# State-space stage: GpSimd's work for a quarter of the channels dealt out over the tiles ahead of it, and ScalarE's copies of output matrices placed behind the next tile's inputs

## The chip, the cores and the metric

The kernel runs on one core of one Trainium2 chip, in one launch. The metric is the device time in microseconds (us). The core has five engines with a queue each: TensorE (PE in the rows, PEld its weight loads), VectorE (DVE), ScalarE (ACT), GpSimd (POOL) and SyncE (SP), which issues most of the transfers.

## The reference, cut to what matters

Two layers on x (256 positions, 2048 channels). The first layer's token mixer is a state-space model (S5): 128 groups of 16 channels, each with 64 complex states.

```python
a_bar = exp(lam * dt)
b_bar = ((a_bar - 1) / lam) * b_mat
bu = einsum('btgi,gpi->btgp', u, b_bar)
h  = scan of  h[t] = a_bar * h[t-1] + bu[t]
y  = real(einsum('btgp,gip->btgi', h, c_mat))
y  = gelu(y + d_skip * u);  vg = y @ w_glu
...
mod = silu(c) @ ada_w[i] + ada_b[i]        # six conditioning vectors for each layer
x = layer_norm(ALPHA*x + (1+gate)*sublayer(x*(1+scale)+shift))
```

A SwiGLU feed-forward follows, then a second layer with a convolution mixer in place of S5. Only the S5 part is touched by the change.

## The kernel before, in words

The 2048 channels are 16 tiles of 128 channels (`ct`), in 4 quarters of 4 tiles. The state-space stage is a loop over the tiles, pipelined by hand over three of them. Iteration `ct` does these things in program order:

- `weights_in(ct+1)`: ScalarE copies input matrices (`mb`, L376), TensorE transposes them (`btr`, L384), ScalarE copies the result (`lz`, L385).
- `ada_units`: TensorE multiplies 1 MB units of the conditioning weights that stream in (`ada`, L613). `plan` gives a tile 2, 3 or 4 units; they stand between the other steps. A finished block of four units is copied (`adas`, L616) and turned (`adat`, L620).
- `tables(ct+1)`: ScalarE copies a tile's part of the quarter's table `tq` into `tab` (L358), and GpSimd doubles it once more (L349).
- `read_out(ct-1)`: TensorE computes `y` (L476 to L487) from the state that VectorE left (`pc`, `psn`).
- `inputs(ct+1)`: TensorE transposes x (`xt`), ScalarE applies the conditioning (`uh` and `u`, L930) and last scales X (L1297). `drive(ct+1)`: TensorE multiplies `uh` into `pin` (L421).
- `weights_out(ct+1)`: five ScalarE instructions, one `dd` (L393) and four that copy the output matrices `qc` into `mc` (L396, L397, two each); then TensorE's `bdp` (L399, L403), which reads them, and ScalarE's `bd` (L407). `mc` and `dd` have three buffers.
- `scan(ct)`: VectorE's chain over `pin` (L438 to L471), with the gelu of tile ct-1 between its steps: ScalarE L1304, VectorE L1307, ScalarE L1308, VectorE L1312 (`gl`), ScalarE L1313 (`h`), GpSimd L1314.
- GpSimd's work for the next quarter, queued behind its own last instruction of `tables(ct+1)`. `matrices(q)` has three steps (L311), each of four multiplications and two sums over 128x256; the first makes `qb` for `weights_in`, the other two `qc` for `weights_out`. `quarter(q)` makes `tq` in five doublings j = 0 to 4 (L349), each twice as wide as the one before.

TensorE's instructions run in the order of the program (a manual schedule). On the other engines the build's scheduler chooses the order among instructions whose inputs it holds ready, and the order is fixed in the program. `issue_after(ins)` places what a block issues on that instruction's engine behind it in the queue; it is not a wait for its end. Each engine's queue runs in its order.

In the kernel before, `matrices(1)` takes one step in each of the iterations 0, 1 and 2, and `quarter(1)` is issued whole behind the second step. For quarters 2 and 3 the steps stand in iterations 3, 4, 5 and 7, 8, 9, and the whole `quarter` behind the third step, in iterations 5 and 9. The `weights_out` instructions of ScalarE stand behind the X scaling of tile 0 alone (`first`).

Of the kernel before, what the change touches and what calls it, by code (L numbers as in the profile page):

```python
# [153 lines left out]
class S5:  # L154
# [170 lines left out]
    def quarter(self, q, eng):  # L325

        t = self.tq[q] = self.keep.tile([P, 2, 16, 32], F32, tag="tq", name="tq", bufs=2)
        sl = slice(16 * q, 16 * q + 16)
        for r in range(2):
            eng.memset(t[:, r, :, 0:1], 1.0 - r)  # L330
        xt, yt = (self.keep.tile([P, 2, 16, 16], F32, tag=n, name=n) for n in ("xq", "yq"))
        for j in range(5):
            self.double(t, self.wt[:, j, :, sl], j, xt, yt, 16, eng)

    def double(self, t, w, j, xt, yt, npair, v):

        n = 1 << j
        src = t[:, :, :, 0:n]
        if n == 1:
            src, xs, ys = t[:, :, :, 0], xt[:, :, :, 0], yt[:, :, :, 0]  # L340
            f = [bc(w[:, r, :], 1, 2) for r in range(2)]
        else:
            xs, ys = xt[:, :, :, 0:n], yt[:, :, :, 0:n]
            f = [bc(bc(w[:, r, :], 1, 2), 3, n) for r in range(2)]
        parts = [(xs, src, f[0], MUL), (ys, src, f[1], MUL),
                 (t[:, 0, :, n:2 * n], xt[:, 0, :, 0:n], yt[:, 1, :, 0:n], SUB),
                 (t[:, 1, :, n:2 * n], xt[:, 1, :, 0:n], yt[:, 0, :, 0:n], ADD)]
        for out, a, b, op in parts:
            last = v.tensor_tensor(out=out, in0=a, in1=b, op=op)  # L349
        return last  # L350
# [143 lines left out]
def kernel(  # L494
# [9 lines left out]
    nc = tc.nc  # L504
# [6 lines left out]
    def aux(name):  # L511
        return auxp.tile([P, 512], F32, tag="aux", name=name)
# [31 lines left out]
    s5 = S5(tc, const, ident, auxp, "aux", pin_ctx.enter_context(tc.tile_pool(name="pin", bufs=2, space=PSUM)))  # L544
# [51 lines left out]
    def queue_behind(instructions):  # L596

        st = ExitStack()
        for i in instructions:
            st.enter_context(tc.issue_after(i.ins))  # L600
        return st
# [629 lines left out]
    def ada_units(n):  # L1231
        nonlocal block
        for _ in range(n):
            ada_turn()
            if not block:
                if not parts:
                    return
                block = [ada_block(0, *parts.pop(0)), 0]
            next(block[0])
            block[1] += 1  # L1240
# [6 lines left out]
            ada_units(1)  # L1247
    for _ in s5.matrices(0, nc.vector):
        pass
    s5.quarter(0, nc.vector)  # L1250
    s5_prep.close()
    s5.start_work()
    w = s5.work
# [1 line left out]
    def load_x(q):  # L1255
        for t in range(2):
            nc.sync.dma_start(
                X.rearrange("c k (t p) -> c k t p", t=2)[:, 4 * q:4 * q + 4, t],
                x[0].rearrange("(c two) (k p) -> two c k p", two=2, p=P)[t][:, 4 * q:4 * q + 4])
# [3 lines left out]
    d_col, cb_col, cg_col, cnb_col = (vec[:, 16 * i:16 * i + 16] for i in range(4))  # L1263
# [6 lines left out]
    def half_mod(q):  # L1270
        while len(parts) > 12 - 2 * q or block and len(parts) == 12 - 2 * q and block[1] < 4:
            ada_units(1)
        ada_turn()
        s4 = slice(4 * q, 4 * q + 4)
        b = aux("hmod")
        for h in range(2):
            nc.tensor.matmul(b[:, 8 * h:8 * h + 8], s5.sel[:, 2 * h:2 * h + 2].rearrange("p a t b -> p (a t b)"), mod[0][:, 0:2, s4], start=h == 0, stop=h == 1)
        return nc.scalar.copy(out=hmod[:, :, :, s4], in_=b[:, 0:16].rearrange("p (h j k) -> p h j k", h=2, j=2))

    def inputs(ct):  # L1280

        b = aux("xt")
        xc = X[:, ct].rearrange("c (t p) -> c t p", t=2)
        for t in range(2):
            nc.tensor.transpose(b[:, t * P:(t + 1) * P], xc[:, t], ident)
        for h in range(2):
            for i in range(4):
                o, a = 64 * h + 32 * (i // 2), 32 * i
                nc.tensor.matmul(b[a:a + 32, (2 + h) * P:(3 + h) * P], xc[:, i % 2, o:o + 32], ident, start=True, stop=True)
        if ct % 4 == 0 and ct:  # L1290
            half_mod(ct // 4)
        u = w.tile([P, SEQ], F32, tag="u", name="u", bufs=3)
        uh = w.tile([P, 2, HALF], F32, tag="uh", name="uh", bufs=2)
        for h in range(2):
            affine(uh[:, h], b[:, (2 + h) * P:(3 + h) * P], hmod[:, h, 1, ct:ct + 1], hmod[:, h, 0, ct:ct + 1])
        affine(u, b[:, :SEQ], mod[0][:, 1, ct:ct + 1], mod[0][:, 0, ct:ct + 1])
        return u, uh, nc.scalar.mul(X[:, ct], b[:, :SEQ], ALPHA)  # L1297
# [18 lines left out]

        return first, second, third

    extra = s5.matrices(1, nc.gpsimd)
    tabs, held, coming = {}, None, None  # L1320
    more = ExitStack()
    raws[:] = [rawp] * 4 + [more.enter_context(tc.tile_pool(name="raw5", bufs=2))] * 2
# [2 lines left out]
    def start_dense():  # L1325
        nonlocal const2, wp
        const2 = ctx.enter_context(tc.tile_pool(name="const2", bufs=1, reuse_waits="tile"))
        wp = mctx.enter_context(tc.tile_pool(name="w", bufs=2, reuse_waits="tile"))
        ready.append(Unit(wp, s5_w_glu[0], 0, 4, [(0, 256), (D, 256)]))
# [3 lines left out]
    def scan(ct, now, y):  # L1333

        nonlocal held
        turns = list(gelu(*held[:2], y)) if held else []

        def between():
            if turns:
                turns.pop(0)()  # L1340

        held = ct, now[1], *s5.scan(ct, now[2], tabs.pop(ct), between)
        while turns:
            between()

    with tc.manual_schedule(engines={mybir.EngineType.PE}):
        half_mod(0)
        first = None
        for ct in range(-1, NCH - 1):
            now, y = coming, None  # L1350
            if (ct + 1) % 4 == 1 and ct < 12:
                load_x(ct // 4 + 1)
            s5.weights_in(ct + 1)
            n = plan[ct + 1]
            ada_units(n > 0 and ct >= 0)
            tabs[ct + 1] = s5.tables(ct + 1)
            if held:
                y = s5.read_out(*held)
            u, uh, last = inputs(ct + 1)
            first = first or last  # L1360
            ada_units(n > 1 and ct >= 0)
            coming = ct + 1, u, s5.drive(ct + 1, uh)
            s5.weights_out(ct + 1, d_col[:, ct + 1:ct + 2], first)
            ada_units(n - 2 if ct >= 0 else n)
            if ct == NCH - 2:
                raws[:] = [rawp]
                more.close()
                s5.keep_ctx.close()
                start_dense()
            if ct < 0:  # L1370
                continue
            scan(ct, now, y)
            if ct % 4 == 3 and ct < 11:
                extra = s5.matrices(ct // 4 + 2, nc.gpsimd)
            with queue_behind([s5.last]):
                next(extra, None)
                if ct % 4 == 1 and ct < 12:
                    s5.quarter(ct // 4 + 1, nc.gpsimd)
    accp = None

    def last_scan():
# [57 lines left out]
    with mctx:  # L1439
# [18 lines left out]
        first = {"acc": [b.rearrange("p (a b) -> p a b", b=SEQ) for b in (aux("acc"), bank)], "before": {1: last_scan, 2: lambda: held_back.append(s5.end), 3: s5_end}}  # L1458
# [180 lines left out]
```

## Time and profile before

| | |
|---|---|
| runs | 2353.70, 2355.54, 2361.51 us; median 2355.54 us |
| profiled execution | 2354.07 us, of which the span from first to last instruction is 2352.3 us |
| mean granted TensorE clock | 0.986 of full |
| the stage's VectorE chain, first instruction of tile 0 to last of tile 14 | 48.80 to 232.84 us, 184.04 us |

The span is the part of the time that the rows can show. The stage is less than a tenth of it; matrix products with streamed weights follow up to the end.

### The profile page before, as it was taken

To read this page: it belongs to the slowest core of one execution; us is meant where nothing else is said; L and a number is where in the kernel's file an instruction comes from. 1 tells how busy PE (TensorE), PEld (TensorE's weight loads), DVE (VectorE), ACT (ScalarE), POOL (GpSimd) and SP (SyncE) were. 2 spreads that over 40 slices of the span, in tenths; PEclk is the share of its full clock that TensorE was granted. 3 is DMA by queue.
4 is the path that set the end of the run, shared out by engine and by line. 5 is a ranking of instruction groups with operands and counts; after the bars stand their busy time and mean duration, and the time that the engine had idled before them with its cause. 6 is when DMAs were issued, how large, how long until landed. Compare 5 with 4: busy or idle time off the path is not lost.

```text
span 2352.3 us, 34010 instructions
## 1 busy us (share of the span) xinstructions
PE 2264.1 (96%) x13837; PEld 1825.5 (78%) x13837; DVE 1643.2 (70%) x1790; ACT 1014.1 (43%) x1239; POOL 227.7 (10%) x290
## 2 busy tenths in 40 slices
PE   6788999999999999999999999899999999999999
PEld 4454877888888888888887767797888888888888
DVE  8889988878777777777885555888755544454564
ACT  4566334553433333433453322556434333344343
POOL 2673000200000000000031101402000000000000
PEclk9899999999999999999999999999999999999998
DMA  9678799588888898988746776775875555555542
GB/s 349 239 266 303 257 338 350 166 283 307 305 307 305 315 315 295 322 304 308 276 146 202 222 230 209 274 242 163 281 235 189 187 186 189 188 188 182 194 162 89
DMA packets 378546, 580.29 MB, mean 247 GB/s; under 512 B 14835, under 2 KB 272163, under 8 KB 363923
## 3 DMA queue, kind: packets, MB, share of 16 engines
q1 hardware_dynamic: 377958, 577.68, 71.6%
q8 instruction: 108, 1.77, 0.3%
q0 software_dynamic: 192, 0.37, 0.1%
q14 instruction: 48, 0.39, 0.0%
q10 hardware_dynamic: 240, 0.08, 0.0%
HBM read 567.83 MB, written 2.10 MB: 242 GB/s over the span
## 4 chain that ended last, share of the span: by engine, by line
PE 75%; issue 7%; DVE 6%; POOL 6%; ACT 3%; DMA 3%; SPq 1%; POOLq 0%; DVEq 0%; ACTq 0%
PE acc L869 64%; PE acc L873 3%; PE conv L1535 2%; DVE wlo L816 2%; PE turned L885 2%; ACT whi L815 1%; POOL h L967 1%; DMA raw<-in_cv_w_pw_dram 1%; POOL mu L311 1%; DMA raw<-in_s_w_glu_dram 1%; SPq L1518 1%; DVE adaacc L684 1%; POOL tq L349 0%; DVE pin L450 0%; POOL hf L1574 0%
## 5 line engine op out<-in xcount | busy, mean ns | idle before, releaser
L816 DVE TENSOR_TENSOR wlo<-raw,whi 128x2048 fp32r<-128x2048 f32 x344 | 797.5, 2319 | 507.4 <-ACT whi L815 490.6
L815 ACT CAST whi<-raw 128x2048 fp32r<-128x2048 f32 x344 | 654.9, 1904 | 829.2 <-PE acc L869 561.4
L869 PE MATMUL acc<-whi,h 128*128 128x512 f32 x3648 | 899.7, 396 | 15.9 <-ACT whi L815 15.3
L869 PEld LDWEIGHTS acc<-whi,h 128*128 128x128 f32 x3648 | 681.2, 189 | 176.9 <-ACT whi L815 24.4
L869 PE MATMUL acc<-wlo,h 128*128 128x512 f32 x1824 | 465.6, 393 | 3.6 <-DVE wlo L816 3.6
L869 PEld LDWEIGHTS acc<-wlo,h 128*128 128x128 f32 x1824 | 343.0, 188 | 80.8 <-DVE wlo L816 5.9
L869 PE MATMUL acc<-whi,f 128*128 128x512 f32 x1248 | 300.5, 391 | 0.0
L684 DVE SCALAR_TENSOR_TENSOR adaacc<-rawa,c_act,adaacc 128x2048 f32<-128x2048 f32 (+1 forms) x135 | 287.1, 2127 | 0.4
L869 PEld LDWEIGHTS acc<-whi,f 128*128 128x128 f32 x1248 | 233.2, 188 | 48.8 <-ACT whi L815 0.8
L869 PE MATMUL acc<-wlo,f 128*128 128x512 f32 x624 | 156.5, 389 | 0.0
L869 PEld LDWEIGHTS acc<-wlo,f 128*128 128x128 f32 x624 | 117.2, 188 | 24.2
L1507 POOL TENSOR_TENSOR lw<-fold,wtap 128x1024 f32<-128x1024 f32 x16 | 35.6, 2229 | 897.4 <-PE acc L873 710.6
L967 POOL TENSOR_TENSOR h<-hf,h 128x512 fp32r<-128x512 f32 x24 | 48.2, 2016 | 329.9 <-ACT h L966 322.6
L613 PE MATMUL ada<-raw,c_rep 128*32 128x512 f32 x512 | 72.9, 659 | 6.7 <-DVE c_rep L559 4.8
L1192 ACT ACTIVATE fsg<-acc 128x256 f32<-128x256 f32 x84 | 31.9, 380 | 104.5 <-PE acc L869 104.5
L873 PEld LDWEIGHTS acc<-h,whi 128*128 128x128 f32 x512 | 62.3, 190 | 9.5 <-DVE h L1564 2.9
L1138 POOL CAST lnmh<-lno 128x2 fp32r<-128x2 f32 x1 | 0.2, 182 | 713.8 <-DVE lno L65 713.8
L873 PE MATMUL acc<-h,whi 128*128 128x256 f32 x512 | 66.3, 285 | 2.8 <-DVE h L1564 2.0
L1535 PE MATMUL conv<-vs,lw 128*32 128x256 f32 x1024 | 62.8, 380 | 0.0
L1535 PEld LDWEIGHTS conv<-vs,lw 128*32 128x32 f32 x1024 | 41.7, 109 | 16.6 <-issue 3.5
L1193 DVE TENSOR_TENSOR fsg<-acc,fsg 128x256 f32<-128x256 f32 x84 | 35.3, 420 | 19.9 <-ACT fsg L1192 19.8
L450 DVE TENSOR_TENSOR_SCAN pin<-rho,pin 128x256 f32<-128x256 f32 x64 | 44.3, 692 | 1.3
(334 smaller groups left out, 1853.4 us busy)
## 6 DMA issues: line engine op xcount, KB each, us to landing
raw<-in_ffn_w_gu_dram SPq DMA_DIRECT2D x352, 512.0 KB, 4.4
rawa<-in_ada_w_dram SPq DMA_DIRECT2D x128, 1024.0 KB, 5.6
raw<-in_ffn_w_down_dram SPq DMA_DIRECT2D x88, 1024.0 KB, 5.0
raw<-in_ada_w_dram SPq DMA_DIRECT2D x64, 1024.0 KB, 7.3
raw<-in_s_w_glu_dram SPq DMA_DIRECT2D x64, 512.0 KB, 5.9
raw<-in_cv_w_pw_dram SPq DMA_DIRECT2D x64, 512.0 KB, 4.9
raw<-in_cv_w_pw_dram SPq DMA_DIRECT2D x16, 1024.0 KB, 5.5
vs<-pad SPq DMA_DIRECT2D x112, 71.0 KB, 2.1
```

What stands on the lines that cost most here:

```text
L450: v.tensor_tensor_scan(out=z, data0=rh[:, a].rearrange("p r h c -> p (r h c)"), data1=z, initial=0.0, op0=MUL, op1=ADD)
L613: nc.tensor.matmul(acc[32 * k:32 * k + 32, :], c_rep[:, 4 * u + k, :], r[:, k, :], start=u == 0, stop=u == 3)
L684: nc.vector.scalar_tensor_tensor(out=acc, in0=r[:, i], scalar=c_act[:, kk:kk + 1], in1=acc, op0=MUL, op1=ADD)
L815: m1 = nc.scalar.copy(out=self.hi[:, :kn], in_=r[:, :kn])
L816: m2 = nc.vector.tensor_tensor(out=self.lo[:, :kn], in0=r[:, :kn], in1=self.hi[:, :kn].bitcast(F32), op=SUB)
L869: nc.tensor.matmul(acc[bank].rearrange("p a b -> p (a b)"), x[:, bank * HALF:(bank + 1) * HALF], wt[:, k], start=first, stop=end)
L873: nc.tensor.matmul(acc[bank][:, i], wt[:, k, m * P:(m + 1) * P], x, start=first and i == 0, stop=end and i == 1)
L885: nc.tensor.transpose(b[:, o:o + HALF], u[t][:, c0 + k * P:c0 + (k + 1) * P], ident)
L967: nc.gpsimd.tensor_tensor(out=hl[:, s2], in0=h, in1=hh[:, s2].bitcast(F32), op=SUB)
L1193: nc.vector.tensor_tensor(out=t[:, i], in0=gv[:, 0], in1=t[:, i], op=MUL)
L1507: nc.gpsimd.tensor_tensor(out=lw, in0=fold32.unsqueeze(1).unsqueeze(1).broadcast_to([P, 4, CONV_G, 32]), in1=bc(wtap[:, :, 4 * ch:4 * ch + ...
L1535: nc.tensor.matmul(acc[32 * q:32 * q + 32, :], lw[:, q, g, :], vs[:, q, 4 * g:4 * g + SEQ], start=g == 0, stop=g == CONV_G - 1)
```

## The change

`quarter` becomes a generator that stops after each doubling. A new generator, `quarter_steps(q)`, deals out the three matrix steps `m` and the five doublings `t`. For quarters 2 and 3 this is over four iterations: m; m; m and three doublings; the last two doublings. For quarter 1 it is over three iterations: two m; m and three doublings; two doublings. Besides, `weights_out(ct+1)` now stands behind the X scaling of its own tile's inputs (`last`), where it stood behind that of tile 0. No instruction is added or taken away.

```diff
--- before.py
+++ after.py
@@ -331,6 +331,7 @@
         xt, yt = (self.keep.tile([P, 2, 16, 16], F32, tag=n, name=n) for n in ("xq", "yq"))
         for j in range(5):
             self.double(t, self.wt[:, j, :, sl], j, xt, yt, 16, eng)
+            yield
 
     def double(self, t, w, j, xt, yt, npair, v):
 
@@ -1247,7 +1248,8 @@
             ada_units(1)
     for _ in s5.matrices(0, nc.vector):
         pass
-    s5.quarter(0, nc.vector)
+    for _ in s5.quarter(0, nc.vector):
+        pass
     s5_prep.close()
     s5.start_work()
     w = s5.work
@@ -1316,7 +1318,15 @@
 
         return first, second, third
 
-    extra = s5.matrices(1, nc.gpsimd)
+    def quarter_steps(q):
+
+        m, t = s5.matrices(q, nc.gpsimd), s5.quarter(q, nc.gpsimd)
+        for steps in ((m,), (m,), (m, t, t, t), (t, t)) if q > 1 else ((m, m), (m, t, t, t), (t, t)):
+            for g in steps:
+                next(g)
+            yield
+
+    extra = quarter_steps(1)
     tabs, held, coming = {}, None, None
     more = ExitStack()
     raws[:] = [rawp] * 4 + [more.enter_context(tc.tile_pool(name="raw5", bufs=2))] * 2
@@ -1345,7 +1355,6 @@
 
     with tc.manual_schedule(engines={mybir.EngineType.PE}):
         half_mod(0)
-        first = None
         for ct in range(-1, NCH - 1):
             now, y = coming, None
             if (ct + 1) % 4 == 1 and ct < 12:
@@ -1357,10 +1366,9 @@
             if held:
                 y = s5.read_out(*held)
             u, uh, last = inputs(ct + 1)
-            first = first or last
             ada_units(n > 1 and ct >= 0)
             coming = ct + 1, u, s5.drive(ct + 1, uh)
-            s5.weights_out(ct + 1, d_col[:, ct + 1:ct + 2], first)
+            s5.weights_out(ct + 1, d_col[:, ct + 1:ct + 2], last)
             ada_units(n - 2 if ct >= 0 else n)
             if ct == NCH - 2:
                 raws[:] = [rawp]
@@ -1371,11 +1379,9 @@
                 continue
             scan(ct, now, y)
             if ct % 4 == 3 and ct < 11:
-                extra = s5.matrices(ct // 4 + 2, nc.gpsimd)
+                extra = quarter_steps(ct // 4 + 2)
             with queue_behind([s5.last]):
                 next(extra, None)
-                if ct % 4 == 1 and ct < 12:
-                    s5.quarter(ct // 4 + 1, nc.gpsimd)
     accp = None
 
     def last_scan():
```

## Rows read from the trace of the kernel before

**Rows 1.** By stretch: us; busy PE, PEld, DVE, ACT, POOL; PEclk; DMA share; GB/s

```profile
48.80:232.84 184.04, 150.41 (x2251) 88.59 (x2251) 160.43 (x338) 118.95 (x349) 103.36 (x203) 0.93 0.79 277
...
287.00:411.00 124.00, 121.24 (x548) 94.06 (x547) 105.54 (x89) 49.57 (x46) 0.00 (x0) 1.00 0.99 343
```

**Rows 2.** Waits of VectorE in the stage: us in total, times, longest us

```profile
DVE gl L1312 <- ACT u L1308: 8.9, 3, 8.5
...
DVE u L1307 <- ACT u L1304: 5.0, 8, 1.3
...
DVE x L438 <- POOL tab L349: 3.6, 2, 1.8
...
DVE gl L1312 <- POOL h L1314: 0.4, 2, 0.2
```

**Rows 3.** VectorE in order of time (start us, us) around its longest wait

```profile
75.35 1.42 DVE L450 TENSOR_TENSOR_SCAN pin<-rho,pin 128x256 f32<-128x256 f32 x2
...
85.29 0.42 DVE L1312 TENSOR_TENSOR gl<-u,y 128x256 f32<-128x256 f32 x1 [8.52 <-ACT u L1308]
```

**Rows 4.** ScalarE in order of time over the same stretch

```profile
72.17 0.38 ACT L1304 ACTIVATE u<-y 128x256 f32<-128x256 f32 x1
...
81.90 0.63 ACT L397 ACTIVATE mc<-qc 64x128 f32<-64x128 f32 x2 [9.36 <-POOL qc L311]
...
82.89 0.80 ACT L930 ACTIVATE uh<-xt,hmod 128x128 f32<-128x128 f32 x2
...
84.04 0.37 ACT L1297 ACTIVATE X<-xt 128x256 f32<-128x256 f32 x1
...
84.77 0.43 ACT L1308 ACTIVATE u<-u 128x256 f32<-128x256 f32 x1
```

**Rows 5.** GpSimd in order of time, second quarter's work and the doublings

```profile
51.83 2.36 POOL L311 TENSOR_TENSOR mu<-cm,par 128x256 f32<-128x256 f32 x4
...
60.42 0.61 POOL L349 TENSOR_TENSOR xt<-tab,wt 128x256 f32<-128x256 f32 x1 [4.85 <-ACT tab L358]
...
62.52 2.36 POOL L311 TENSOR_TENSOR mu<-cm,par 128x256 f32<-128x256 f32 x4
...
66.19 0.17 POOL L330 MEMSET tq<- 128x16 f32 x2
...
70.30 0.63 POOL L349 TENSOR_TENSOR xq<-tq,wt 128x256 f32<-128x256 f32 x1
...
74.71 1.41 POOL L349 TENSOR_TENSOR tq<-xq,yq 128x256 f32<-128x256 f32 x2
...
81.15 1.40 POOL L311 TENSOR_TENSOR qc<-mu,mu 128x256 f32<-128x256 f32 x2
```

**Rows 6.** GpSimd's table and VectorE's wait for it, in the third quarter

```profile
133.97 0.87 POOL L349 TENSOR_TENSOR tab<-xt,yt 128x128 f32<-128x128 f32 x2
...
134.46 0.69 DVE L438 TENSOR_TENSOR x<-pin,tab 128x512 f32<-128x512 f32 x1 [1.79 <-POOL tab L349]
```

**Rows 7.** ScalarE's first tile: start of the five copies, and what follows them

```profile
47.72 0.41 ACT L393 ACTIVATE dd<-ident,vec 128x128 f32<-128x128 f32 x1
...
49.26 0.41 ACT L358 COPY tab<-tq 128x256 f32<-128x256 f32 x1
```

**Rows 8.** TensorE in order of time: transposes of tile 3, `drive` of tile 4

```profile
72.36 0.64 PE L1289 MATMUL xt<-ident,X 128*32 128x128 f32 x16
...
96.82 1.16 PE L421 MATMUL pin<-uh,lz 64*128 64x128 f32 x16
```

**Rows 9.** Busy time by stretch, two tiles with four conditioning units each

```profile
206.99:218.89 11.90, 10.04 (x164) 5.81 (x160) 10.62 (x24) 8.05 (x23) 2.80 (x5) 1.00 0.99 358
...
218.89:229.86 10.97, 10.08 (x164) 5.81 (x160) 10.50 (x25) 5.58 (x17) 3.26 (x6) 1.00 1.05 355
```

**Rows 10.** A small VectorE sum: duration ns min/median/max

```profile
L461 DVE TENSOR_TENSOR cx<-cx,cy x16: 149/156/764, 55.5 to 245.7; 128x4 f32<-128x4 f32 x16
```

**Rows 11.** The load queue's waits in the stage

```profile
SPq L570 <- PE ada L613: 157.8, 44, 14.8
```

## The prediction

> **What bounds the kernel now.** I read the busy time by stretch first. In the stage, VectorE is busy for 160.43 us of 184.04, TensorE for 150.41, ScalarE for 118.95, GpSimd for 103.36 [rows 1]. So VectorE leads with little to spare, TensorE is close behind, and what the stage can give back is VectorE's idle time, 23.6 us. The second view is who VectorE waited for [rows 2]. One wait stands out: 8.5 us of the 8.9 us in which `gl` (L1312) waited for ScalarE's L1308. Next come 5.0 us for L1304 in eight pieces, and 3.6 us in two waits for GpSimd's table. The small rest of the idle time is spread over the gaps between instructions, which the change doesn't touch.
>
> The third view is the order of time around the long wait. VectorE has nothing between the scan that ends at 76.77 and L1312 at 85.29 [rows 3]. ScalarE, which it waits for, stood still from 72.55 to 81.90, and its row names the releaser: the copy `mc` (L397) waited for GpSimd's `qc` (L311) [rows 4]. Behind that copy in ScalarE's queue stood `uh` of tile 3, which TensorE and all the rest wait for, and L1308, which had been ready for long. The copy was for tile 4, one tile ahead of what was needed. And GpSimd was late because its order was two matrix steps, the whole quarter from 66.19 to 76.12, a table, and only then the third matrix step, whose sums start at 81.15 [rows 5]. So a copy that nobody needed yet held up everything behind it.
>
> In quarters 2 and 3 the matrix steps came early enough, but the whole quarter stood in front of a table: GpSimd's two last table instructions start at 133.97, VectorE's `x` waits 1.79 us for them [rows 6]. The pattern stands twice, which gives the 3.6 us.
>
> **The change part by part.** All is set against the profiled execution, 2354.07 us; the median of the runs is 1.47 us above it.
>
> *The long wait, minus 8.5 us.* A matrix step takes GpSimd 3.7 us (62.52 to 66.19, [rows 5]). With two in iteration 0, GpSimd works from 51.83 to about 59.2, and the next table can't start before 60.42 anyway: the pair is free. The third step then follows at 62.5 and ends near 66.2, some 16 us earlier than now. The first three doublings take 66.19 to 70.30, 4.1 us, the last two 70.30 to 76.12, 5.8 us. Tile 3's table then starts when ScalarE has copied its input, just ahead of L1304 in its queue, near 72.4, and takes 2.1 us (60.42 to 62.52). The last two doublings end near 80.3, before tile 4's table is due: that waits for VectorE's tile 2, which after 76.77 still has another scan of 1.42 us [rows 3], its small sums and four turns, so not before 80.3 either, by estimate. ScalarE goes from L1304, done at 72.55, to `uh` when its transposes are there, which the wait didn't hold: 72.36 plus 0.64, 73.0 [rows 8]. From the start of `uh` to the end of X it is 82.89 to 84.41, 1.5 us [rows 4], so X ends near 74.5. The five copies, now behind it, take 1.5 us (47.72 to 49.26, [rows 7]) and L1308 0.43 us: done by 76.6. VectorE asks for it at 76.77. So the whole 8.52 us go, and either half of the change removes most of this wait alone: what would be late next is the other half's wait, some 2 us for the table, which GpSimd finishes now near 78.9 (76.12, one other instruction and the 2.1 us).
>
> *The two table waits, minus 3.6 us.* With two of the five doublings put behind the table, GpSimd is 5.8 us earlier at it, against a wait of 1.79. `pin` isn't late there. With it go the two waits for GpSimd's L1314, minus 0.4 [rows 2], which stood behind the same doublings.
>
> *Copies no longer ahead of L1304 and `uh`, minus 1.3 us.* Copies for a tile ahead stand between `y` and L1304 and cost up to 0.3 us in about half of the tiles. Bounds: nothing, and all of the 5.0 us that VectorE waits for L1304 [rows 2]. Most of the 5.0 is TensorE's own lateness with `y`, so I take a quarter.
>
> *Copies ahead of L1308, plus 1.5 us.* Behind X the five copies are older in the program than L1308 and will stand before it, 1.5 us, of which `uh` and X gain back some 0.6 by starting earlier. In two tiles L1312 already waits some 0.2 us each for L1308, the rest of the 8.9 us [rows 2]; there VectorE would wait 0.9 us more. I reckon with four tiles of that tight order; the bounds are nothing (VectorE has the next tile's `x` to do instead) and 3.6 us; I take less than half, since the order on VectorE is chosen anew.
>
> *TensorE's `bdp` waits for the copies, plus 1.5 us.* The copies were done a tile ahead; now `bdp` stands in TensorE's fixed order right behind `drive`. From the end of `uh` (82.89 plus 0.80) to that of X it is 0.72 us, the copies 1.5, and `drive` hides 1.16 [rows 8]: TensorE idles 1.1 us in each tile, and behind it stand the conditioning units, the next transposes and `y`. With two or three units a tile TensorE has at least that much idle time, in which it waits for VectorE; there it costs nothing while VectorE leads. In tiles 12 to 15, with four units, TensorE is busy 10.04 of 11.90 and 10.08 of 10.97 us [rows 9], so 0.9 to 1.9 us are there to hide 1.1 plus what already waits on ScalarE. I take 0.4 us for each of four tiles; the bounds are nothing and 1.1 each, 4.4.
>
> *The port of GpSimd and VectorE, nothing.* A tiny VectorE sum, L461, takes 149 ns at best and 764 at worst [rows 10], L460 ahead of it likewise; the long ones fall where GpSimd is at work. GpSimd's work for a quarter spreads into a fourth tile, but the whole quarter already ran over into that tile, so I count no change; the bounds are a gain and a loss of 1.2 us for each of three tiles, 3.6. The Trainium skill's page "SBUF — State Buffer", section "Who interferes with whom", says that a VectorE instruction with two inputs in SBUF and a GpSimd instruction that reads SBUF lock each other out for a whole instruction. The trace agrees, with 764 ns against 149; by that rule work on more tiles costs more, which is the third rival below.
>
> Sum: -8.5 - 3.6 - 0.4 - 1.3 + 1.5 + 1.5 = -10.8 us, 2343.3 by the profiled execution, 2344.7 by the median. What follows the stage passes it on: the load queue spends 157.8 us of the stage waiting for TensorE to free buffers [rows 11], so the loads come earlier with the work. The stretch from 287 to 411 us, with transfers at 0.99 of the engines' time [rows 1], starts earlier as a whole.
>
> **The rivals.**
>
> *TensorE becomes the bound, slower.* If the 1.1 us (1.6 at most: the durations without overlap) at `bdp` counts in each of 15 tiles, it is 16 to 24 us against gains of 13.8. At 1.6 it gives plus 10.2, 2365.7. It breaks even at 0.9 us a tile. For it: TensorE's 150.41 of 184.04, in a fixed order. Against: it now waits for VectorE in most tiles. Chance 0.09.
>
> *The gain is swallowed.* The stretch from 287 us is bound by transfers; were the loads' start set by something other than buffers, or were the new order of VectorE's and ScalarE's queues behind the stage worse by as much, the time would stay, near 2355. Against: rows 11. Also here: the scheduler finds another early instruction that holds ScalarE. Chance 0.14.
>
> *The lock.* Each quarter's extra tile pays 1.2 us: 3.6 less gain, 2348.3. For: the doublings move to where the small sums stand. Against: they were there already. Chance 0.13.
>
> **How the numbers follow.** Forecast 0.64 with 2344.7. A measurement of this kernel tells about 0.3% from no change, 7.1 us, so faster means under 2348.5. The lock rival sits on that line, half of it on either side; a part of the forecast, 0.04, with its losses at their bounds, is also no more than the same. Faster 0.64 - 0.04 + 0.07 = 0.67, same 0.04 + 0.06 + 0.14 = 0.24, slower 0.09. The range: all gains with L1304's whole 5.0 and no loss is -17.5, 2338.0 by the median; gains with losses near their bounds (3.6, 4.4 and a part of 3.6) is about -3, 2352.5. It leaves out slower and the half of the swallowed case.
>
> **What would show it.** ScalarE's L397 shows no wait for GpSimd, and VectorE has no idle time over 2 us between 50 and 220. VectorE's `x` never waits for the table. TensorE's `bdp` has a wait of about 1 us for `mc` in each tile. The stage's chain ends near 222 where it ended at 232.84, and the loads-bound stretch begins as much earlier. I am wrong if `x` or L1312 shows new waits of about a us in most tiles, or if the stage's gain is there and the end doesn't move.

## The result, and the profile after

The changed kernel takes 2342.44 us, median of five runs (2339.14 to 2346.13). Its ratio to the kernel before, run beside it, is 0.9934, 95% interval [0.9917, 0.9952]: faster by 0.7%, 13 us between the medians. The forecast was 2344.7 us, range 2338.0 to 2352.5. The profiled execution of the changed kernel is the slowest of its five (2346.13 us, span 2344.4 us), so its end says less than its stage does.

The stage first, by the same cut as [rows 1], from VectorE's first instruction of tile 0 to its last of tile 14; lines of the changed kernel lie one or two further down (L397 is L398 now, L1304 is L1306, L1308 is L1310, L1312 is L1314).

```profile
48.92:222.95 174.03, 151.31 (x2258) 87.92 (x2259) 162.17 (x338) 116.29 (x350) 104.74 (x204) 0.96 0.87 294
```

174.0 us, where it was 184.0. The engines have about the same work as before; what went is idle time of VectorE, 23.6 us then and 11.9 now. Who VectorE waited for says which, against [rows 2]:

```profile
DVE u L1309 <- ACT u L1306: 4.5, 10, 1.1
...
DVE adasum L624 <- PE adat L621: 2.5, 5, 0.7
DVE gl L1314 <- ACT u L1310: 0.6, 1, 0.6
```

No row of a wait for GpSimd is left: neither for a table nor for `h`. Of the 8.9 us of L1312 for ScalarE, 0.6 stand. VectorE around the place of the long wait, against [rows 3]:

```profile
75.99 1.42 DVE L451 TENSOR_TENSOR_SCAN pin<-rho,pin 128x256 f32<-128x256 f32 x2
...
77.61 0.68 DVE L439 TENSOR_TENSOR x<-pin,tab 128x512 f32<-128x512 f32 x1
...
78.55 0.41 DVE L1314 TENSOR_TENSOR gl<-u,y 128x256 f32<-128x256 f32 x1
```

ScalarE over the same stretch, against [rows 4]:

```profile
73.28 0.39 ACT L1306 ACTIVATE u<-y 128x256 f32<-128x256 f32 x1 [0.81 <-PE y L488]
74.23 0.81 ACT L931 ACTIVATE uh<-xt,hmod 128x128 f32<-128x128 f32 x2 [0.56 <-PE xt L1291]
...
75.38 0.39 ACT L1299 ACTIVATE X<-xt 128x256 f32<-128x256 f32 x1
75.64 0.60 ACT L617 COPY adas<-ada 128x512 f32<-128x512 f32 x1
76.11 0.43 ACT L394 ACTIVATE dd<-ident,vec 128x128 f32<-128x128 f32 x1
...
77.35 0.30 ACT L398 ACTIVATE mc<-qc 64x128 f32<-64x128 f32 x1
77.68 0.42 ACT L1310 ACTIVATE u<-u 128x256 f32<-128x256 f32 x1
```

The copies follow X, none waits for GpSimd, and L1310 stands behind them. It ends at 78.10, when VectorE's scan has been over for 0.7 us; VectorE does not idle, since it takes `x` of the next tile first. It can, because GpSimd has that tile's table ready (against [rows 5]):

```profile
57.98 1.43 POOL L311 TENSOR_TENSOR qc<-mu,mu 128x256 f32<-128x256 f32 x2
61.06 0.61 POOL L350 TENSOR_TENSOR xt<-tab,wt 128x256 f32<-128x256 f32 x1 [1.65 <-ACT tab L359]
...
65.48 1.42 POOL L311 TENSOR_TENSOR qc<-mu,mu 128x256 f32<-128x256 f32 x2
...
73.40 0.87 POOL L350 TENSOR_TENSOR tab<-xt,yt 128x128 f32<-128x128 f32 x2
...
78.61 1.41 POOL L350 TENSOR_TENSOR tq<-xq,yq 128x256 f32<-128x256 f32 x2
```

The third matrix step ends at 66.9 and the table at 74.3. TensorE has the new waits that the prediction spoke of, in total, times and longest:

```profile
PE bdp L404 <- ACT mc L397: 5.5, 11, 0.5
PE y L488 <- DVE pc L439: 5.3, 9, 2.1
PE adat L621 <- ACT adas L617: 4.5, 5, 1.4
PE bdp L400 <- ACT dd L394: 1.9, 5, 0.5
```

With two single waits of 0.6 us put down to GpSimd it is 8.6 us at `bdp` over 15 tiles.

Does what follows move with it? The transfers of the next weights, before and after (duration min/median/max in ns, then first and last start):

```profile
L570 SPq DMA_DIRECT2D raw<-in_s_w_glu_dram x64: 367/478/1571, 218.9 to 403.0; - x64
```

```profile
L571 SPq DMA_DIRECT2D raw<-in_s_w_glu_dram x64: 367/497/1380, 207.9 to 392.9; - x64
```

The first load of that queue comes 11.0 us earlier, the last 10.1. The loads-bound stretch starts earlier as a whole and hands the gain on.

For the experiments one landmark serves in all traces: the start of ScalarE's last L1304 (the first gelu step of tile 15), the last figure of its row. Before and after:

```profile
L1304 ACT ACTIVATE u<-y x16: 376/383/384, 64.0 to 254.9; 128x256 f32<-128x256 f32 x16
```

```profile
L1306 ACT ACTIVATE u<-y x16: 384/385/386, 64.9 to 243.2; 128x256 f32<-128x256 f32 x16
```

254.9 and 243.2: 11.7 us. There is one trace of each kernel, so how far this mark varies between executions is not shown; VectorE's last table instructions ahead of the stage start at 48.3 to 48.8 us in all of them, so a difference of half a us says nothing.

The landmark lies behind the first matrix products of the next part of the kernel (`acc`), and what happens there is in it too. A second mark lies ahead of them: the start of TensorE's `y` of tile 13 (`y<-u,bd`, L476). TensorE runs in the program's order, so the same work stands ahead of it in every kernel here, but for the repeats of `bdp`. Before and after, 11.6 us apart:

```profile
222.72 0.49 PE L476 MATMUL y<-u,bd 128*128 128x129 f32 x2
```

```profile
211.17 0.49 PE L477 MATMUL y<-u,bd 128*128 128x129 f32 x2
```

### The profile page after: what moved, and what is told of

Its sections match the earlier page's. It is cut to its first block, busy times and chain, and to the rows that moved or that the text cites. A ratio compares the mean times of both kernels' runs of the same rounds, so it can differ in the third digit from the quotient of the medians.

```text
span 2344.4 us, 34011 instructions
## 1 busy us (share of the span) xinstructions
PE 2262.0 (96%) x13837; PEld 1822.5 (78%) x13837; DVE 1642.7 (70%) x1790; ACT 1011.0 (43%) x1239; POOL 229.1 (10%) x290
## 4 chain that ended last, share of the span: by engine, by line
PE 74%; DVE 8%; issue 6%; DMA 5%; ACT 4%; POOL 2%; SPq 1%; DVEq 0%; ACTq 0%; POOLq 0%
PE acc L870 64%; PE acc L874 3%; DMA raw<-in_cv_w_pw_dram 2%; PE conv L1541 2%; DVE wlo L817 2%; PE turned L886 2%; DMA raw<-in_s_w_glu_dram 1%; ACT whi L816 1%; POOL h L968 1%; DVE pin L451 1%; PE y L488 1%; DVE adaacc L685 1%; PE ada L614 1%; DMA raw<-in_ada_w_dram 1%; DVE x L439 0%
## 5 line engine op out<-in xcount | busy, mean ns | idle before, releaser
L1194 DVE TENSOR_TENSOR fsg<-acc,fsg 128x256 f32<-128x256 f32 x84 | 35.3, 420 | 19.9 <-ACT fsg L1193 19.8
```

The costliest lines, as they stand in the source:

```text
L1194: nc.vector.tensor_tensor(out=t[:, i], in0=gv[:, 0], in1=t[:, i], op=MUL)
```

## The experiments

All of them in one table; the ratios are to the kernel before, run on the same chip beside each. Its median was 2355.54 us beside the change, 2358.58 beside the first four experiments, 2355.33 beside the next four and 2355.68 beside the last three, so the rows are compared by their ratios and not by their medians.

| kernel | `y` of tile 13, us | landmark, us | median, us | ratio to before, 95% |
|---|---|---|---|---|
| before | 222.7 | 254.9 | 2355.54 | |
| the change | 211.2 | 243.2 | 2342.44 | 0.9934 [0.9917, 0.9952] |
| GpSimd's spread alone | 213.3 | 247.1 | 2342.66 | 0.9939 [0.9925, 0.9953] |
| copies behind their own inputs alone | 213.3 | 245.3 | 2340.86 | 0.9934 [0.9921, 0.9948] |
| the change, `bdp` later | 207.6 | 243.5 | 2342.36 | 0.9938 [0.9926, 0.9951] |
| the change, small sums into PSUM | 209.2 | 241.2 | 2339.29 | 0.9921 [0.9908, 0.9935] |
| spread in quarters 2 and 3 alone | 218.6 | 250.8 | 2348.69 | 0.9973 [0.9962, 0.9984] |
| copies of tile 4 alone | 213.1 | 245.3 | 2346.06 | 0.9956 [0.9941, 0.9970] |
| before, small sums into PSUM | 221.3 | 255.1 | 2353.95 | 0.9987 [0.9979, 0.9995] |
| the change, `bdp` later, sums into PSUM | 204.3 | 239.0 | 2339.72 | 0.9925 [0.9911, 0.9939] |
| copies alone, sums into PSUM | 209.3 | 241.3 | 2340.62 | 0.9937 [0.9922, 0.9953] |
| the change, `bdp` three times | 216.1 | 248.4 | 2343.59 (one run) | |
| the change, `bdp` twice | 211.2 | 243.2 | 2343.75 (one run) | |

**Each half alone.** First GpSimd's spread with the copies where they were:

```diff
+        first = None
...
+            first = first or last
...
-            s5.weights_out(ct + 1, d_col[:, ct + 1:ct + 2], last)
+            s5.weights_out(ct + 1, d_col[:, ct + 1:ct + 2], first)
```

> Only GpSimd's work is dealt out; the output-matrix copies stay behind tile 0's inputs, a tile ahead. Landmark for all runs: the start of the last gelu square on ScalarE in the stage, 254.92 us in the kernel before and 243.2 in the changed one. Theory (GpSimd's lateness was the cause of all three long waits, and placing the copies gives about nothing net): VectorE's 8.5 us wait and both 1.79 us waits for the table are gone, the landmark stands at 242 to 245, and the time is 12 us under the kernel before, 2341 to 2345. Rival (the copies' place was the main part): a long wait of ScalarE's copy for GpSimd stays, the landmark is at 248 or later, and the time is within 5 us of the kernel before.

Then the copies with GpSimd's work as before:

```diff
-        first = None
...
-            first = first or last
...
-            s5.weights_out(ct + 1, d_col[:, ct + 1:ct + 2], first)
+            s5.weights_out(ct + 1, d_col[:, ct + 1:ct + 2], last)
```

> Only the copies are placed behind their own tile's inputs; GpSimd's order stays as in the kernel before. Theory: the 8.5 us wait of VectorE shrinks to some 2 us, now for the table that GpSimd finishes near 79; the two waits of 1.79 us stay; the landmark stands at 248 to 250 and the time is 5 to 7 us under the kernel before, 2349. Rival (the copies' place was the main part): the landmark is at 245 or earlier. Rival (GpSimd alone decides): the long wait stays at 7 us or more, the landmark is near 254.

With the spread alone all three waits are gone; the landmark is 247.1, between the theory's band and the rival's; what is lost against the whole change goes partly to L1304, for which VectorE waits 6.1 us in all where it waits 4.5 in the changed kernel. With the copies alone the long wait has become one of 1.44 us, for the table, and the two waits of 1.79 us, which I expected to stay, are gone too. VectorE in that kernel, at the long wait's place and at that of the first of the two:

```profile
78.53 0.69 DVE L438 TENSOR_TENSOR x<-pin,tab 128x512 f32<-128x512 f32 x1 [1.44 <-POOL tab L349]
...
126.47 1.42 DVE L450 TENSOR_TENSOR_SCAN pin<-rho,pin 128x256 f32<-128x256 f32 x2
127.81 0.67 DVE L438 TENSOR_TENSOR x<-pin,tab 128x512 f32<-128x512 f32 x1
```

And GpSimd's table there:

```profile
126.29 0.88 POOL L349 TENSOR_TENSOR tab<-xt,yt 128x128 f32<-128x128 f32 x2
```

The table is done at 127.17. The new order has put `x` behind the tile's second scans, at 127.81; in the kernel before it stood ahead of them and came too early [rows 6]. So the halves are not terms of a sum: 7.8 and 9.6 us of the landmark alone, 11.7 together; 9.5 and 9.4 by `y` of tile 13, 11.6 together; and in the time no difference between them.

**The copies of one tile.** The kernel before, with the five copies of tile 4 alone moved:

```diff
-            s5.weights_out(ct + 1, d_col[:, ct + 1:ct + 2], first)
+            s5.weights_out(ct + 1, d_col[:, ct + 1:ct + 2], last if ct == 3 else first)
```

> The kernel before with one edit: the five copies of output matrices of tile 4 alone stand behind the X scaling of their own tile's inputs; those of all other tiles, and all of GpSimd's work, as before. Theory (one copy, a tile early, held all of ScalarE's queue): the 8.5 us wait shrinks to some 1.4 us for the table, the two waits of 1.79 us for tables in quarters 2 and 3 stay; the last gelu square at 247.8 us (254.9 less 7.1), or 246 if VectorE's new order hides those two as well; the time 2346 to 2348. Rival (the gain of the copies' new place comes from all sixteen tiles, the long wait being only where it shows): the landmark at 251 or later, the time over 2350.

The landmark is 245.3, the same as with the copies of all tiles and 0.7 us beyond the better end of the theory, and the time is 2346.06 us, as the theory had it. VectorE's wait at the old place, and a later one:

```profile
78.82 0.69 DVE L438 TENSOR_TENSOR x<-pin,tab 128x512 f32<-128x512 f32 x1 [1.11 <-POOL tab L349]
...
175.01 0.69 DVE L438 TENSOR_TENSOR x<-pin,tab 128x512 f32<-128x512 f32 x1 [1.13 <-POOL tab L349]
```

8.5 us have become 1.1. Of the two other waits one is left, with 1.13 us. The cause of the long wait is shown: these five copies, a tile ahead of need, in ScalarE's queue in front of `uh` of tile 3.

**The other side of it: only the quarters without the long wait.** Quarter 1's order as before, quarters 2 and 3 spread, copies as before:

```diff
-for steps in ((m,), (m,), (m, t, t, t), (t, t)) if q > 1 else ((m, m), (m, t, t, t), (t, t)):
+for steps in ((m,), (m,), (m, t, t, t), (t, t)) if q > 1 else ((m,), (m, t, t, t, t, t), (m,)):
...
+        first = None
...
+            first = first or last
...
-            s5.weights_out(ct + 1, d_col[:, ct + 1:ct + 2], last)
+            s5.weights_out(ct + 1, d_col[:, ct + 1:ct + 2], first)
```

> Quarter 1's work on GpSimd in the order of before (one step; one step and the whole quarter; one step), quarters 2 and 3 spread as in the changed kernel, ScalarE's copies placed as before. Theory (the long wait of 8.5 us comes from quarter 1's order alone, the two waits of 1.79 us from the whole quarter ahead of the table): VectorE's wait of about 8.5 us near 77 us is there as before, no wait for a table is left; the last gelu square of the stage at about 251 us (254.9 before, less 3.6), the time 2350 to 2353. Rival one (the two table waits are swallowed by the order of VectorE's work, as they vanished with the copies moved alone): the landmark at 253.5 to 255, the time as before. Rival two (the gain comes from the calmer later quarters and not from the long wait): the landmark at or under 248, the time near 2343.

VectorE's waits:

```profile
DVE gl L1314 <- ACT u L1310: 9.0, 3, 8.6
DVE u L1309 <- ACT u L1306: 5.0, 8, 1.4
```

The long wait is back and no table is waited for. The landmark is 250.8: 4.1 us earlier, against 3.6 for the tables and 0.4 for `h` [rows 2]. The time is a little under the expected band, by 1.3 us.

**TensorE at `bdp`.** In the changed kernel, `bdp`, with ScalarE's `bd` that reads it, is put behind the conditioning units that followed it:

```diff
+    def bdp(self, ct):
...
             s5.weights_out(ct + 1, d_col[:, ct + 1:ct + 2], last)
             ada_units(n - 2 if ct >= 0 else n)
+            s5.bdp(ct + 1)
```

> The changed kernel, with TensorE's bdp product moved behind the conditioning units that follow it, so that TensorE no longer stands still for the copies. In the changed kernel these waits are 8.6 us in the stage. Theory (VectorE leads, TensorE's waits at bdp cost only in tiles with four units): the waits at bdp fall under 2 us, the landmark moves by 0 to 2 us earlier, the time by less than 3 us. Rival (TensorE is the bound by now): the landmark moves by 5 us or more.

TensorE's waits at `bdp` fall from 8.6 to 2.2 us, and the time and the landmark, 243.5 against 243.2, stay as they were. But the stage moves: `y` of tile 13 starts 3.6 us earlier.

```profile
207.57 0.49 PE L481 MATMUL y<-u,bd 128*128 128x129 f32 x2
```

The lead is lost at the first products with the next part's weights, for which TensorE stands still until ScalarE has made `whi` of them. With `bdp` later and, below it, in the changed kernel:

```profile
218.55 6.73 PE L874 MATMUL acc<-whi,h 128*128 128x512 f32 x16 [3.03 <-ACT whi L820]
```

```profile
221.26 3.71 PE L870 MATMUL acc<-whi,h 128*128 128x512 f32 x15 [0.75 <-ACT adas L617]
```

By stretch, with `bdp` later (busy PE is the first figure behind the length, the granted clock the third from the end) and, below it, in the changed kernel:

```profile
215.00:218.50 3.50, 0.52 (x18) 0.36 (x18) 3.50 (x7) 3.39 (x8) 2.97 (x6) 0.90 1.06 322
218.50:225.30 6.80, 6.75 (x17) 5.35 (x18) 6.01 (x6) 1.79 (x1) 4.50 (x8) 0.55 0.68 193
```

```profile
221.20:225.00 3.80, 3.74 (x16) 3.11 (x17) 3.80 (x4) 2.13 (x3) 2.23 (x3) 1.00 0.81 230
```

TensorE was busy for 0.52 of 3.50 us ahead of these products, and the clock granted for them was 0.55, close to the lower of its two levels (1.2 of 2.4 GHz), where the changed kernel has 1.00. So the landmark hides this gain. From `y` of tile 13 to that of tile 14 it is 15.9 us in the changed kernel and 19.8 here; in three other kernels it is long too, 17.7 with the spread alone, 17.7 in the kernel before with the small sums into PSUM, and 18.6 with `bdp` later and the sums into PSUM. Next, more work at that place instead of less: the products of `bdp` made again, from the start, into the same bank.

```diff
         bk = self.bank("bdp")
+        for _ in range(3):
-        nc.tensor.matmul(bk[:, 0:32], dd, self.fold, start=True, stop=False)
+            nc.tensor.matmul(bk[:, 0:32], dd, self.fold, start=True, stop=False)
...
```

> The changed kernel with the TensorE products of bdp made three times over into the same bank, each time from the start, so that the result is the same: 1.5 us more of TensorE's work in each tile (0.735 us once), right behind the copies, some 22 us over the stage's 15 tiles, which is about all of TensorE's idle time in it (174.0 less 151.3). Theory (VectorE sets the pace and TensorE's idle time covers work of this size in most tiles): the last gelu square at 243 to 252 us. The rival of the prediction (what TensorE does at bdp counts in full): 265 us.

(The label says twice; this kernel makes them three times.) And twice:

> The changed kernel with the TensorE products of bdp made twice, 0.735 us more in each tile, 11 us over the stage. Theory: the last gelu square within 2 us of 243.2. Rival (it counts in full): 254 us; a half of it, 248.7, would mean that TensorE sets the pace in half of the tiles.

The same stretch of time with three and, below it, with two (with three, the stage runs on behind it); TensorE's busy time is the first figure behind the length:

```profile
48.90:223.00 174.10, 160.98 (x2778) 100.24 (x2776) 162.00 (x335) 112.53 (x344) 103.19 (x202) 0.97 0.85 287
```

```profile
48.90:223.00 174.10, 156.81 (x2546) 94.88 (x2546) 164.89 (x338) 116.89 (x350) 104.89 (x205) 0.97 0.87 293
```

Twice costs nothing at either mark, 243.2 and 211.2; three times costs 5.2 and 4.9 us of some 22 that were added. With two, the products of `bdp` take 9.9 us more in this stretch (21.7 for 11.8), and those of `y` 4.1 us less (39.6 for 43.7). That doubling is free is not shown by this, though: from `y` of tile 10 to that of tile 13, where each iteration has four units, it is 33.41 us with `bdp` later, 34.88 in the changed kernel, 36.25 with two and 36.96 with three, half a us a tile for the first two steps. In the tiles ahead of these the order on VectorE differs between the kernels, and single tiles differ by up to 4 us either way. Both kernels ran once, so their times only say that nothing large happened.

**The port of VectorE and GpSimd.** In the changed kernel, the two small sums whose inputs both lay in SBUF add into `pin`, which lies in PSUM (the same numbers, added in another order):

```diff
-        v.tensor_tensor(out=cx[:, :, 0], in0=cx[:, :, 0], in1=cy[:, :, 1], op=ADD)
-        v.tensor_tensor(out=cx[:, :, 1], in0=cx[:, :, 1], in1=cy[:, :, 0], op=SUB)
         first = pin[:, :, 1, :, :, 0]
         v.tensor_tensor(out=first, in0=first, in1=cx, op=ADD)
+        v.tensor_tensor(out=first[:, :, 0], in0=first[:, :, 0], in1=cy[:, :, 1], op=ADD)
+        v.tensor_tensor(out=first[:, :, 1], in0=first[:, :, 1], in1=cy[:, :, 0], op=SUB)
```

> The changed kernel, with the two small VectorE sums L461 and L462, which read two operands in SBUF, replaced by two that read one operand in PSUM (the sum is taken into pin at once, in another order of additions); the same number of instructions. Theory of the lock (a VectorE instruction with two SBUF inputs stands still while GpSimd reads): the durations of the replacements lie at 150 to 180 ns with none over 250, where the sums took up to 770; VectorE is 4 to 5 us less busy in the stage and the landmark moves by 1 to 4 us earlier. Rival (the small sums are long for another reason, such as the instruction ahead of them): single durations of 400 ns and more stay, and the landmark moves by less than 1 us.

These sums in the changed kernel (ns min/median/max):

```profile
L461 DVE TENSOR_TENSOR cx<-cx,cy x16: 154/188/760, 55.0 to 234.3; 128x4 f32<-128x4 f32 x16
...
L462 DVE TENSOR_TENSOR cx<-cx,cy x16: 150/156/770, 55.6 to 234.4; 128x4 f32<-128x4 f32 x16
```

and with the edit:

```profile
L463 DVE TENSOR_TENSOR pin<-pin,cy x16: 160/170/171, 55.1 to 232.9; 128x4 f32<-128x4 f32 x16
...
L464 DVE TENSOR_TENSOR pin<-pin,cy x16: 160/170/171, 55.3 to 233.1; 128x4 f32<-128x4 f32 x16
```

No long one is left, and both marks are 2.0 us earlier. The 32 sums take 5.4 us where they took 9.0, 3.6 less against 4 to 5 expected. The same edit in the kernel before:

> The kernel before with one edit: the two small sums of VectorE that had both inputs in SBUF (L460, L461) add into pin in PSUM instead, so that one input of each is in PSUM; the same numbers are added in another order. Theory (the long durations are a lock between VectorE and GpSimd that an operand in PSUM avoids, whatever the order of GpSimd's work): all durations of these sums 150 to 180 ns, their busy time 5.4 us where it was 10.5; the 8.5 us wait stays; the last gelu square 2 to 5 us earlier than 254.9, at 250 to 253, the time 2350 to 2354. Rival (the sums' long durations fall where VectorE would wait anyway, so removing them gives nothing without the change): the landmark at 254 to 255, the time as before.

The sums are short there too, and the landmark stays at 255.1, as the rival had it. `y` of tile 13 comes 1.4 us earlier, though, and the interval of the ratio (0.9979 to 0.9995) lies just below 1: the whole time fell by 1 to 5 us. VectorE's waits, against [rows 2]:

```profile
DVE gl L1312 <- ACT u L1308: 11.3, 4, 8.6
DVE u L1307 <- ACT u L1304: 5.2, 7, 1.4
...
DVE x L438 <- POOL tab L349: 2.5, 1, 2.5
```

The long wait is as long as before, the others for L1308 grew by 2.3 us, and of the 5.1 us that the sums gave (10.5 to 5.4) the stage kept 1.4. Most of the time saved ahead of a wait whose end others set is not saved.

**Combinations.** `bdp` later and the sums into PSUM, on top of the change:

> The changed kernel with both later edits: bdp behind the conditioning units that follow it in TensorE's order, and the two small sums into pin in PSUM. Theory (TensorE's waits at bdp are covered even when VectorE is 2 us faster): the last gelu square at 241 us as with the sums alone (241.2), the time 2337 to 2341. Rival (with VectorE faster the waits at bdp begin to set the pace): the landmark at 238 to 240 us, the time 2 to 3 us under that of the sums alone.

The landmark is 239.0, 2.2 us earlier than with the sums alone, as the rival had it, and `y` of tile 13 is 4.9 us earlier; the time doesn't show it (ratios 0.9925 and 0.9921). And the copies and the sums, without GpSimd's spread:

> The kernel before with ScalarE's copies behind their own tile's inputs and the two small sums into pin in PSUM; GpSimd's work whole, as before. Theory (once the copies are moved, GpSimd's spread is worth only what the last waits for tables cost, and sums of 0.16 us give their gain where no long wait takes it back): the last gelu square near 243 us (245.3 with the copies alone, less 2), the time 2338 to 2341, not told apart from the changed kernel with these sums (2339.3). Rival (the spread is needed: faster sums make VectorE ask for the tables earlier, and it waits for them): waits for tables of 4 us or more in all, the landmark at 245 or later, the time 2341 or more.

The landmark is 241.3, where the whole change with these sums has 241.2, and one wait of 1.6 us for a table stands: once the copies are moved and the sums are short, GpSimd's spread adds nothing that either mark shows. The kernels with ratios of 0.9921 to 0.9939, the change among them, can't be told from each other by their times: all their intervals overlap.

## Why the prediction was right, step by step

*The long wait, minus 8.5 us.* Right in size and cause: one edit to one tile's copies takes it away, and where quarter 1 keeps its old order it is back with 8.6. The order of time on GpSimd came as worked out (third step done at 66.9 for 66.2, table started at 72.13 for 72.4, last doublings done at 80.0 for 80.3). On ScalarE L1310 was done at 78.10, not at 76.6: X ended 1.3 us later than worked out, and an `adas` copy came between. That was covered by VectorE's `x`, which the step had named as a bound for the copies ahead of L1308, not here. "Either half alone removes most" is right as well, and what is late next is the table, with 1.44 us for some 2.

*The table waits, minus 3.6 us.* Right in size (250.8 in the kernel with nothing else), incomplete in cause: the copies alone remove them too, through another order on VectorE. So the terms of this sum overlap, and it comes out near the truth because each wait was counted once.

*Copies ahead of L1308, plus 1.5 us:* from 0.4, the rest beside the long wait, to 0.6; over-sized by 1.3, since VectorE found `x` to do. *L1304, minus 1.3 us, and `bdp`, plus 1.5 us.* VectorE's rows don't part these two, since it waits for L1304 and for `adat`, both, when TensorE is late. Together they were to give plus 0.2; the wait for L1304 fell from 5.0 to 4.5 us and that for `adat`, which the sum does not name, rose from 1.6 to 2.5, plus 0.4. The wait at `bdp` is 0.57 us a tile, not 1.1, but the term for its cost was not too large: with `bdp` later the same two waits of VectorE come to 2.7 us up to the end of tile 14, where the changed kernel has 7.0, and `y` of tile 13 is 3.6 us earlier, against 1.5 taken and bounds up to 4.4. Where an iteration has four units it is half a us a tile, where 0.4 was taken; the rest lies in the tiles ahead, where the step had it hidden, and is less sure, as the order on VectorE differs there. If so, the gain at L1304 was larger than 0.5, too, by how much is not shown; that the two nearly cancelled as forecast is luck in part.

*The port, nothing.* The two sums' busy time in the stage fell by 1.5 us, 10.2 to 8.6, inside the bounds of 3.6. The Trainium skill's page "SBUF — State Buffer", section "Who interferes with whom", says that outside its two-port modes a VectorE instruction with at most one input in SBUF does not contend with GpSimd; the traces agree, with 171 ns at most where it was 770. The rival of the lock fell, though: dealing GpSimd's work over more tiles didn't lengthen the sums in the changed kernel. With the spread alone they did lengthen, 12.3 us over all tiles where the kernel before has 10.5; so their cost seems to hang on where they happen to fall.

*From the waits to the stage.* VectorE's waits fell by 11.9 us: the 10.8 of the sum, and the 1.3 less the 0.2 above. The stage fell by 10.0; most of the rest stands in VectorE's busy time, which grew from 160.4 to 162.2 although the small sums took less. VectorE's instructions did not get slower on the whole: their durations add up to 177.8 us before and 177.2 after. Neighbouring ones overlap in the rows and the busy time counts an overlap once, so there is less overlap; why, I did not settle.

*The end.* The stage gave 10.0 us against 10.8 predicted, and the medians differ by 13.1, interval of the ratio 11 to 20 us. Runs of one kernel spread by 3 to 13 us, so the difference alone says little. But in all ten kernels with a ratio the time gained more than the landmark, by 1 to 7 us; where that comes from stays open, and that the median lies so close below the forecast is luck as far as this goes. TensorE as the bound and the swallowed gain are both shown wrong, the first by `bdp` later (3.6 us of the stage, not 16 to 24), the second by the loads, 10 to 11 us earlier.

## What to carry to other kernels

Ask of a long wait what stands behind the waiting instruction in its queue: here the copies for a tile ahead of need cost 8.5 us of the stage, and moving that one tile's copies gave 9.6 of the change's 11.7 us, some 2.5 of it through shorter waits for tables. Two remedies of one wait don't add, and a new order on another engine can remove waits that nobody touched; try each alone before both are kept. Test a feared cost both ways, by more of it and by less, and read the result ahead of the next thing that can wait: here doubling the products at `bdp` left both marks where they were, and the landmark didn't move with the waits gone either, but `y` of tile 13 came 3.6 us earlier.

## What was not expected of the hardware

A VectorE sum over 128x4 elements takes 156 to 188 ns at the median in the changed kernel and up to 770 ns where GpSimd is at work; with the spread alone the longest took 1012 ns, in the two kernels with more work at `bdp` 1022 and 1035 ns. In the kernel before, all ten from 193 us on, behind GpSimd's work for the last quarter, take 0.16 us. GpSimd's longest single instructions in this stage's doublings are of 1.06 and 0.74 us. With one input in PSUM instead of SBUF the small sum takes 171 ns at most in each of four kernels. In the kernel before that took 5.1 us off these sums, and the stage kept 1.4 us of it while the long wait stood behind them.

TensorE's first 16 products behind a stand of 3.03 us took 6.73 us at a granted clock of 0.55, where the changed kernel's 15 took 3.71 us at 1.00.
